# Single-engine steps for attention pieces, row and weight preparation, and PSUM read-outs

## The chip, the core and the metric

The kernel runs on one core of a Trainium2 chip. The metric is the device time of one execution in microseconds (us). A core has TensorE (PE in the profile, its weight loads PEld), VectorE (DVE), ScalarE (ACT), GpSimd (POOL) and SyncE (SP), which here only issues DMAs.

## The reference

2048 tokens of width 1024 go through one layer:

```python
h = rmsnorm(x, attn_norm_w)
q_a, k_a, v_a, q_b, k_b, v_b, g_b, g_c, x_c = split(h @ w_in)   # 1024 -> 3072
y_sb = stick_breaking_attention(q_a, k_a, v_a)                  # 4 heads of 64
y_ch = chunked_relpos_attention(rmsnorm(q_b), rmsnorm(k_b), v_b, rel_bias)   # 8 heads, band of 576 keys
y_cv = g_b * causal_conv3(g_c * x_c)                            # 256 channels
x = x + group_rmsnorm([y_sb, y_ch, y_cv], out_norm_w) @ w_out
x = x + (silu(h2 @ w_gate) * (h2 @ w_up)) @ w_down              # h2 = rmsnorm(x, ffn_norm_w), 2816 wide
```

Stick-breaking attention weights key s by `sigmoid(z_ts)` times the product of `1 - sigmoid(z_tj)` over the keys between s and t; with the sequence stored in reverse order that product is one running product along the keys.

## The kernel before

**Products.** Every projection is made of three half-precision products per 128 rows of the contraction (`mm3`, L320 to L322: high x high, high x low, low x high), in units of 8 x 3 matmuls into an `acc` bank of PSUM (two banks). A weight is two tiles `wr` of 128x1024. `Weights.load` issues their DMAs on SP's queue and, right behind each in ScalarE's program, a Square with a sum (L183) that bounds the tile's size. `Weights.split` adds the sums up on PE (L206 or L208, two small matmuls `ones`), makes a power-of-two scale on VectorE (L212 to L220), and then, for both tiles, scales on ScalarE (L225), casts to the high half (L226), subtracts on GpSimd for the low half (L227), and stores both halves to DRAM (L231). `get` is called when a weight is wanted: it calls `split` of the next weight and `load` of the one after it, in one go.

**Rows.** `Rows.ahead` makes two row blocks of 128 tokens after each other: load, Square (L310), a chain of 11 small VectorE operations (L312 and `rsqrt`, L103 to L116), a multiplication by scale and gain (L314), eight transposes on PE into two `sc` banks (L275, three banks), each read by ScalarE (`hh`, L277) and VectorE (`hl`, L278).

**Attention.** Each of 12 heads is cut into pieces. A piece of stick-breaking attention has three stages: `front` makes scores on PE (L608 to L611), two sigmoids on ScalarE (`be` L634, `re` L635), the running product on VectorE (L636) and a multiplication (L638); `mid` (`transposed`) transposes the result on PE into a `tp` bank (L574, two banks) and reads it by ScalarE (`wth`, L576) and VectorE (`wtl`, L577); `back` multiplies by V into the one `av` bank (L587, L592), which `put_y` reads by ScalarE (L599) and GpSimd adds up (L600). A piece of chunked attention has a maximum (L636's place is taken by L670, L674), an exponential (L676) and a reciprocal (L679, L680). `finish` in `chunk_qk` and `conv_block` transposes into `tp` too (L517, L554).

**Order.** The sequence is cut into two halves. `weave` writes the first 1210 us by hand: `run` takes projection steps from `fill` and counts their cost on a clock; `stage` calls, for one piece after another, `mid` of the piece 3 before, `back` of the piece 5 before and `front` of the piece itself, with a third of a gap of projection steps behind each. `later(t, f)` calls f once the clock has moved by t. In this part PE's order is the written order (`manual_schedule`). The order on VectorE, ScalarE, GpSimd and SP is made by the framework's scheduler from the program as it was written. `y_norm` (L739 to L745) normalizes the first half's attention output between 600 and 760 us. Behind `weave` come the FFN of the first half, the second half's output projection and the second half's FFN; they are not interleaved with attention.

Of the kernel before, what the change touches and what calls it, by code (L numbers as in the profile page):

```python
# [18 lines left out]
D = 1024  # L19
# [21 lines left out]
def trunk(ctx: ExitStack, tc: tile.TileContext, x, anw, w_in, qnw, knw, biasx, conv_w, onw, w_out,  # L41
# [44 lines left out]

    def acc():
        return ps.tile([128, 512], F32, name="acc", tag="acc", bufs=2)

    def sc1():  # L90
        return ps.tile([128, 512], F32, name="sc", tag="sc", bufs=3)

    def tpb():
        return ps.tile([128, 512], F32, name="tp", tag="tp", bufs=2)
# [66 lines left out]
    class Weights:  # L161
# [3 lines left out]
        def __init__(self, plan):  # L165
            self.plan = plan
            self.raw, self.ready = {}, {}
            self.at = 0

        def load(self, n):  # L170
            if n >= len(self.plan) or n in self.raw or self.plan[n] in wd:
                return
            key = self.plan[n]
            shape, one, gain, srcs = block(key)
            ss = small(2, "ws", BF16)
            tiles = []
            for i, unit in enumerate(srcs):
# [7 lines left out]
            self.raw[n] = ss, tiles  # L185

        def split(self, n):
            if n >= len(self.plan) or n in self.ready:
                return
            key = self.plan[n]  # L190
            shape, one, gain, srcs = block(key)
# [9 lines left out]
            ss, tiles = self.raw.pop(n)  # L201
            m = len(tiles)
            o = tpb()
# [5 lines left out]
            c = 1 if one else m  # L209
# [10 lines left out]
            nc.vector.tensor_scalar(ds[:, :c], ds[:, :c], INV[gain], None, op0=ALU.mult)  # L220
            DS[key] = ds, one
            made = []
# [6 lines left out]
            wd[key] = [dp.tile([128, 2, D], F16, name=f"wd{len(wd)}_{i}") for i in range(m)]  # L229
            for w, t in zip(made, wd[key]):  # L230
                nc.sync.dma_start(t, w)  # L231
            self.ready[n] = made

        def ahead(self):
            self.split(self.at)
            self.load(self.at + 1)

        def get(self, key):
# [4 lines left out]
            self.split(n)  # L243
# [23 lines left out]
    def to_T(xn, hh, hl, t):  # L267

        cs = slice(t * 128, (t + 1) * 128)
        for i in range(2):  # L270
            p = sc1()
# [4 lines left out]
            pk = p.rearrange("p (k c) -> p k c", k=4)  # L276
            nc.scalar.copy(hh[:, ks, cs], pk)  # L277
            nc.vector.tensor_tensor(hl[:, ks, cs], pk, hh[:, ks, cs], ALU.subtract)  # L278
            yield 0.45

# [25 lines left out]
    def rms_rows(xt, gain, xo=None):  # L306

        xo = xt if xo is None else xo
        ss = small(1, "ss")
        nc.scalar.activation(junk(), xt, AF.Square, accum_out=ss)  # L310
        a = small(1, "sa")
        nc.vector.tensor_scalar(a, ss, -0.5 / D, -0.5 * EPS, op0=ALU.mult, op1=ALU.add)  # L312
        r = rsqrt(a, 1, "rr")
        nc.vector.scalar_tensor_tensor(xo, xt, r, gain, op0=ALU.mult, op1=ALU.mult)  # L314
        return xo
# [45 lines left out]
    class Rows:  # L361


        def __init__(self, H, groups, make):
            self.H, self.make = H, make
            self.todo = [(g, t) for g in groups for t in (0, 2)]
            self.made = set()
            self.patient = False

        def ahead(self):  # L370
            if self.todo:
# [3 lines left out]
                for b in (t, t + 1):  # L375
                    yield from to_T(self.make(g, b), *self.H[g], b)
# [16 lines left out]
    def x_rows(H, groups):  # L393
        gain = []

        def make(g, b):
# [3 lines left out]
            if not gain:  # L400
                gain.append(gain_row("a"))
            return rms_rows(xt, gain[0])

        return Rows(H, groups, make)

    def y_rows(H, groups):
        def make(g, b):
# [4 lines left out]
        return Rows(H, groups, make)  # L412

    def proj_T(H, groups, u, use, between=None):

        wh, wl = u
        for g in groups:
# [3 lines left out]
            o = acc()  # L421
            yield from mm3(o, lambda k: wh[:, k, :], lambda k: wl[:, k, :], lambda k: hh[:, k, :],
                           lambda k: hl[:, k, :], KT)
            use(g, o)

    def proj_N(H, groups, units, use, prep=None):

        for g in groups:
            hh, hl = H.get(g, (None, None))
            for t in range(0, 4, 2):  # L430
# [3 lines left out]
                o = acc()  # L434
# [6 lines left out]
                use(g, t, o)  # L441
# [45 lines left out]
    def chunk_qk(H, groups, W, pair):  # L487
# [25 lines left out]
        def finish(g, w, both):  # L513
            tp = tpb()
# [3 lines left out]
            put_parts(tp, 2 + pair, g, (qd, kd)[w], nw[:, w:w + 1])  # L518

        yield from proj_N(H, groups, units, use)  # L520

    def conv_block(H, groups, W, b, between=None):
# [28 lines left out]
        def finish(g, t1):  # L551
            tp = tpb()
# [3 lines left out]
            nc.scalar.copy(yc[:, :512], tp)  # L556
            for i in range(4):
# [7 lines left out]
    def transposed(src, n):  # L565
# [3 lines left out]
        for b0, b1 in ([(0, 3), (3, 5)] if n == 5 else [(0, n)]):  # L569
            tp = tpb()  # L570
            s = slice(b0 * 128, b1 * 128)
            c = slice(0, (b1 - b0) * 128)
            for b in range(b0, b1):
                nc.tensor.transpose(tp[:, (b - b0) * 128:(b - b0 + 1) * 128],  # L574
                                    src[:, b * 128:(b + 1) * 128], ident)
            nc.scalar.activation(wh[:, s], tp[:, c], AF.Copy, scale=WSC)  # L576
            nc.vector.scalar_tensor_tensor(wl[:, s], tp[:, c], WSC, wh[:, s], op0=ALU.mult,  # L577
# [19 lines left out]
    def put_y(T, head, av, f):  # L597
        u = ap.tile([128, 2 * HD], F32, name="yu", tag="yu")
        nc.scalar.activation(u, av, AF.Copy, scale=f)  # L599
        nc.gpsimd.tensor_tensor(u[:, :HD], u[:, :HD], u[:, HD:], ALU.add)  # L600
        nc.sync.dma_start(ydr[T][:, head * HD:(head + 1) * HD], u[:, :HD])

    def scores(Q, cols, K, k0, n, diagonal=False):

        q1, q2 = Q
        z = sc1()
# [5 lines left out]
        return z[:, :n]  # L612

    def open_av():
        return ps.tile([128, 2 * HD], F32, name="av", tag="av", bufs=1)

    def stick_tile(T, head, K, k0, Q, V, cols):
# [3 lines left out]
        def piece(b, n):  # L621
            N = n * 128
            r = {}

            def front():
                z = scores(Q, cols, K, (b - k0) * 128, N, b == T)
# [6 lines left out]
                r["w"] = be  # L633
                nc.scalar.activation(be[:, :N], z, AF.Sigmoid, scale=ZS[head // 2][:, 0:1])  # L634
                nc.scalar.activation(re, z, AF.Sigmoid, scale=ZS[head // 2][:, 1:2])  # L635
# [3 lines left out]

            def mid():  # L640
                r["T"] = transposed(r["w"], n)

            def back():
# [3 lines left out]
                weighted(av, *r["T"], [V[:, b + i - k0] for i in range(n)], b == T, b + n == NB)  # L647
                if b + n == NB:
                    put_y(T, head, av, VS[head])

            return front, mid, back, n
# [7 lines left out]
    def chunk_tile(T, head, K, k0, Q, V, cols, bias):  # L659
        n = min(5, NB - T)  # L660
        c0 = (T - k0) * 128
        r = {}

        def front():
# [3 lines left out]
            for i, (a, w) in enumerate(parts):  # L668
                z = scores(Q, cols, K, c0 + a, w)
# [4 lines left out]
            nc.vector.tensor_scalar(nm, m[:, 0:1], other, qks[:, 2:3], op0=ALU.max, op1=ALU.mult)  # L674
            tot = small(1, "tot")
            nc.scalar.activation(s[:, :n * 128], s[:, :n * 128], AF.Exp, bias=nm, scale=qks[:, 1:2],  # L676
                                 accum_out=tot)
            f = small(1, "f")
            nc.vector.reciprocal(f, tot)  # L679
            nc.vector.tensor_tensor(f, f, VS[head], ALU.mult)  # L680
            r["s"], r["f"] = s, f
# [364 lines left out]
```

## Time and profile before

| | before |
|---|---|
| median of 3 executions | 2725.04 us (2721.22 to 2729.78) |
| the profiled execution | 2726.58 us |
| span of its trace | 2724.7 us |
| mean granted clock of PE | 0.98 |
| PE busy | 2539.0 us (93%) |
| DVE, ACT, POOL busy | 1467.3, 1079.9, 401.3 us |

The profiled execution's time is 1.9 us above its span. PE's busy time includes matmuls at the lower of its two clocks, which take twice as long. A row of a timeline gives the start in us from the span's start, the duration, the engine, the line and the operation, its output and inputs, and in brackets how long the engine had been idle and what ended that. Tiles are named by the program; a DMA is named by the tiles at its two ends.

### The profile page before, as it was taken

The numbers are of one execution on the slowest core, as the hardware profiler recorded it, in microseconds if no ns is written. First come the engines' busy times: TensorE is split into PE (matmuls) and PEld (weight loads), VectorE is DVE, ScalarE is ACT, GpSimd is POOL, SyncE is SP. The second block draws the span as 40 slices with busy tenths as digits, with TensorE's granted clock in tenths as the row PEclk, the third lists the DMA queues.
The fourth block names the chain that finished last, engine by engine and source line by source line (L and its number), as shares of the span: only waits on it lengthen the run. The fifth ranks groups of instructions, "written<-read, shape, count | busy, mean of one in ns | idle before, by whom it ended". The sixth has DMA issues, their size and how long they took to land.

```text
span 2724.7 us, 41834 instructions
## 1 busy us (share of the span) xinstructions
PE 2539.0 (93%) x16258; PEld 1690.5 (62%) x16258; DVE 1467.3 (54%) x3455; ACT 1079.9 (40%) x1994; POOL 401.3 (15%) x469
## 2 busy tenths in 40 slices
PE   5988888998799888979999999999999999999999
PEld 4567766766687577845555555556865555555556
DVE  6467877789989877844443334334342333223233
ACT  5566756666466777762333333320121111111110
POOL 2124331112313121121111121110000000000000
PEclk8999999999899999989999999999999999999999
DMA  7443435434221256372222223222651111111101
GB/s 246 142 128 97 124 112 159 129 123 146 92 81 47 97 167 194 94 271 102 93 93 93 93 99 110 93 101 98 226 194 39 47 47 49 68 47 47 47 24 62
DMA packets 245352, 294.34 MB, mean 108 GB/s; under 512 B 77472, under 2 KB 194208, under 8 KB 245152
## 3 DMA queue, kind: packets, MB, share of 16 engines
q1 hardware_dynamic: 245152, 291.65, 33.2%
q8 instruction: 128, 2.10, 0.3%
q14 instruction: 72, 0.59, 0.1%
HBM read 199.30 MB, written 92.27 MB: 107 GB/s over the span
## 4 chain that ended last, share of the span: by engine, by line
PE 37%; DMA 5%; issue 4%; DVE 2%; POOL 1%; ACT 1%; SPq 1%; POOLq 0%; DVEq 0%; ACTq 0%
PE acc L321 7%; PE acc L322 7%; PE acc L320 7%; PE sc L963 5%; PE sc L965 5%; PE sc L964 5%; DMA x1d<-xs 2%; DMA wr<-in_w_down 1%; POOL w L227 1%; DMA wr<-in_w_up 1%; PE sc L275 0%; DVE gl L949 0%; DVE wl L260 0%; DVE x L967 0%; ACT wh L258 0%
## 5 line engine op out<-in xcount | busy, mean ns | idle before, releaser
L321 PE MATMUL acc<-hl,w 128*128 128x512 f16 x1728 | 656.1, 380 | 0.2 <-DVE hl L278 0.2
L320 PE MATMUL acc<-hh,w 128*128 128x512 f16 x1728 | 656.2, 380 | 0.0
L322 PE MATMUL acc<-hh,w 128*128 128x512 f16 x1728 | 655.9, 380 | 0.0
L945 DVE SCALAR_TENSOR_TENSOR sg<-acc,ds,sg 128x512 f32<-128x512 f32 x88 | 66.0, 750 | 614.8 <-PE acc L322 539.5
L320 PE MATMUL acc<-w,hh 128*128 128x256 f16 x1408 | 391.6, 278 | 4.0 <-ACT w L226 4.0
L321 PE MATMUL acc<-w,hh 128*128 128x256 f16 x1408 | 391.6, 278 | 1.8 <-POOL w L227 1.8
L322 PE MATMUL acc<-w,hl 128*128 128x256 f16 x1408 | 391.3, 278 | 0.0
L967 DVE TENSOR_TENSOR x<-sc,x 128x512 f32<-128x512 f32 x352 | 241.4, 691 | 211.0 <-PE sc L965 203.6
L322 PEld LDWEIGHTS <-w 128*128 128x128 f16 x1728 | 169.3, 98 | 205.3 <-issue 2.2
L963 PE MATMUL sc<-wh,gh 128*128 128x512 f32 x704 | 282.3, 401 | 4.6 <-DVE x L967 4.5
L320 PEld LDWEIGHTS <-w 128*128 128x128 f16 x1728 | 169.4, 98 | 183.9 <-issue 5.6
L321 PEld LDWEIGHTS <-w 128*128 128x128 f16 x1728 | 169.3, 98 | 180.1 <-issue 0.6
L965 PE MATMUL sc<-wh,gl 128*128 128x512 f32 x704 | 278.0, 395 | 0.0
L964 PE MATMUL sc<-wl,gh 128*128 128x512 f32 x704 | 277.9, 395 | 0.0
L227 POOL TENSOR_TENSOR w<-wr,w 128x1024 f16<-128x1024 f32 x76 | 162.4, 2157 | 547.1 <-ACT w L226 463.9
L577 DVE SCALAR_TENSOR_TENSOR wtl<-tp,wth 128x512 f16<-128x512 f32 (+3 forms) x384 | 200.2, 530 | 46.9 <-ACT wth L576 45.9
L636 DVE TENSOR_TENSOR_SCAN re<-re,zero 128x512 f32<-128x512 f32 (+3 forms) x160 | 187.7, 1173 | 63.2 <-ACT re L635 63.0
L576 ACT ACTIVATE wth<-tp 128x512 f16<-128x512 f32 (+3 forms) x384 | 176.1, 475 | 81.2 <-PE tp L574 80.2
L948 ACT CAST gh<-sg 128x512 fp32r<-128x512 f32 x88 | 54.3, 617 | 384.4 <-DVE sg L945 384.4
L225 ACT ACTIVATE wr<-wr,wsc 128x1024 f32<-128x1024 f32 x76 | 83.4, 1142 | 194.5 <-DVE wsc L216 194.2
L321 PEld LDWEIGHTS <-hh 128*128 128x128 f16 x1408 | 140.5, 100 | 31.5 <-issue 5.7
L963 PEld LDWEIGHTS sc<-wh,gh 128*128 128x128 f32 x704 | 132.5, 188 | 41.3 <-DVE x L967 8.9
(167 smaller groups left out, 3776.2 us busy)
## 6 DMA issues: line engine op xcount, KB each, us to landing
w<-wd SPq DMA_DIRECT2D x92, 512.0 KB, 4.1
wd<-w SPq DMA_DIRECT2D x76, 512.0 KB, 2.7
wr<-in_w_down SPq DMA_DIRECT2D x44, 512.0 KB, 4.4
q<-qd SPq DMA_DIRECT2D x192, 64.0 KB, 2.3
wr<-in_w_gate SPq DMA_DIRECT2D x22, 512.0 KB, 4.4
wr<-in_w_up SPq DMA_DIRECT2D x22, 512.0 KB, 5.4
xt<-in_x SPq DMA_DIRECT2D x16, 512.0 KB, 4.7
wr<-in_w_in SPq DMA_DIRECT2D x16, 512.0 KB, 5.3
```

What stands on the lines that cost most here:

```text
L225: nc.scalar.activation(raw, raw, AF.Copy, scale=sc[:, 0:1] if one else sc[:, i:i + 1])
L227: nc.gpsimd.tensor_tensor(w[:, 1, :], raw, w[:, 0, :], ALU.subtract)
L320: nc.tensor.matmul(o, sh(k), mh(k), start=(k == 0), stop=False)
L321: nc.tensor.matmul(o, sh(k), ml(k), start=False, stop=False)
L322: nc.tensor.matmul(o, sl(k), mh(k), start=False, stop=(k == n - 1))
L576: nc.scalar.activation(wh[:, s], tp[:, c], AF.Copy, scale=WSC)
L577: nc.vector.scalar_tensor_tensor(wl[:, s], tp[:, c], WSC, wh[:, s], op0=ALU.mult, op1=ALU.subtract)
L636: nc.vector.tensor_tensor_scan(re, re, zero.to_broadcast([128, N]), 1.0 if b == T else e[:, 0:1], ALU.mult, ALU.add)
L963: nc.tensor.matmul(o, gh[:, cs], wh[:, cc], start=st, stop=False)
L964: nc.tensor.matmul(o, gh[:, cs], wl[:, cc], start=False, stop=False)
L965: nc.tensor.matmul(o, gl[:, cs], wh[:, cc], start=False, stop=en)
L967: nc.vector.tensor_tensor(x1, o, x1, ALU.add)
```

## The change

Work that `before` wrote in one go is cut into steps, and what is written between two steps comes between them in the program. A piece is one generator, advanced by `beat`; there are three beats for each new piece. A step holds work of one engine at a time: scores, then both sigmoids (now `re` ahead of `be`), then the running product and the multiplication, and so on. A weight's Squares move from `load` to `split`, which has four steps on the clock (`start`, `more`): Squares; 3.0 later the sum, the scale and, 1.5 after that, the first tile; 1.5 later the second tile. The store of a tile follows its low half at once. Rows are loaded a pair ahead (`fetch`), the two blocks of a pair share one chain of scale operations (`rms_rows`, 15 of them for two rows, where there were 2 x 11), and `to_T` reads a bank one step after its transposes. A projection's `acc` bank is read 0.8 later on the clock (`behind`). `y_norm`'s load is issued 5.0 ahead of its work. `bank` hands out PSUM banks and, where the bank it takes has a reader that is not yet written, writes that reader first. The FFN's functions get the same helpers with nothing deferred.

```diff
+    def bank(name, bufs, cols=512):
+        ring = Bank.rings.setdefault(name, [])
+        if len(ring) == bufs:
+            old = ring.pop(0)
+            while not old.done:
+                old.force() if old.force is not None else advance(old.piece)
+        ring.append(Bank())
+        return ps.tile([128, cols], F32, name=name, tag=name, bufs=bufs), ring[-1]
...
         def load(self, n):
...
                 for put, src in unit:
                     nc.sync.dma_start(put(rv), src)
-                with nc.allow_low_precision(reason="a bound, to a factor of two"):
-                    nc.scalar.activation(junk(), raw, AF.Square, accum_out=ss[:, i:i + 1])
...
         def split(self, n):
...
+            for i, raw in enumerate(tiles):
+                with nc.allow_low_precision(reason="a bound, to a factor of two"):
+                    nc.scalar.activation(junk(), raw, AF.Square, accum_out=ss[:, i:i + 1])
+            yield 3.0
+            o, bk = tpb()
...
             for i, raw in enumerate(tiles):
+                yield 1.5
                 w = wp.tile([128, 2, D], F16, name="w16", tag="w16")
                 nc.scalar.activation(raw, raw, AF.Copy, scale=sc[:, 0:1] if one else sc[:, i:i + 1])
                 nc.scalar.copy(w[:, 0, :], raw)
                 nc.gpsimd.tensor_tensor(w[:, 1, :], raw, w[:, 0, :], ALU.subtract)
+                nc.sync.dma_start(wd[key][i], w)
...
+            run_all(self.steps[n])
             self.load(n + 1)
-            if n:
-                self.ahead()
-            else:
-                later(6.0, self.ahead)
+            self.start(n + 1, 2.0)
+            self.load(n + 2)
...
+    def rms_rows(tiles, gain):
+        a = small(2, "sa")
+        for i, xt in enumerate(tiles):
+            nc.scalar.activation(junk(), xt, AF.Square, accum_out=a[:, i:i + 1])
+        yield 0.0
+        nc.vector.tensor_scalar(a, a, -0.5 / D, -0.5 * EPS, op0=ALU.mult, op1=ALU.add)
+        r = rsqrt(a, 2, "rr")
+        for i, xt in enumerate(tiles):
+            nc.vector.scalar_tensor_tensor(xt, xt, r[:, i:i + 1], gain, op0=ALU.mult, op1=ALU.mult)
+        yield 0.0
...
+    def behind(what):
+        if stream.paced:
+            later(0.8, what)
+        else:
+            what()
...
-            use(g, o)
+            behind(bk.read(lambda g=g, o=o: use(g, o)))
...
-    def transposed(src, n):
+    def turned(src, n):
...
+            for b in range(b0, b1):
+                nc.tensor.transpose(tps[-1][0][:, (b - b0) * 128:(b - b0 + 1) * 128],
+                                    src[:, b * 128:(b + 1) * 128], ident)
+        yield
+        for (tp, bk), (b0, b1) in zip(tps, parts):
+            nc.scalar.activation(wh[:, b0 * 128:b1 * 128], tp[:, :(b1 - b0) * 128], AF.Copy, scale=WSC)
+        yield
...
-                nc.scalar.activation(be[:, :N], z, AF.Sigmoid, scale=ZS[head // 2][:, 0:1])
-                nc.scalar.activation(re, z, AF.Sigmoid, scale=ZS[head // 2][:, 1:2])
+                nc.scalar.activation(re, z, AF.Sigmoid, scale=ZS[head // 2][:, 1:2])
+                nc.scalar.activation(be[:, :N], z, AF.Sigmoid, scale=ZS[head // 2][:, 0:1])
+                yield
...
+        def beat(gap):
+            for p in list(line):
+                p[0] -= 1
+                if p[0] == 0:
+                    advance(p)
+            run(clock[0] + gap / 3)
```

In ScalarE's program at the start, the rows below follow the preparation of the first weight. Rows named `xt` with `junk` are the Squares of token blocks 3 to 8 (L310 before, L368 after), `ws` the Square of a weight (L183, now L249), `hh1` the readers of transposed rows. Before:

```order
L226 CAST w16_305<-wr_286 128x1024
L226 CAST w16_309<-wr_290 128x1024
L310 ACTIVATE junk_384,ss_383<-xt_381 128x1024
L465 ACTIVATE vst_377<-acc_328 128x8x64
L277 CAST hh1_206<-sc_400 128x4x128
L277 CAST hh1_206<-sc_407 128x4x128
L183 ACTIVATE junk_439,ws_436<-wr_437 128x1024
L183 ACTIVATE junk_443,ws_436<-wr_441 128x1024
L225 ACTIVATE wr_318<-wr_318,wsc_417 128x1024
L225 ACTIVATE wr_322<-wr_322,wsc_417 128x1024
```

And after:

```order
L275 CAST w16_299<-wr_277 128x1024
L275 CAST w16_304<-wr_279 128x1024
L368 ACTIVATE junk_374,sa_373<-xt_212 128x1024
L368 ACTIVATE junk_376,sa_373<-xt_214 128x1024
L368 ACTIVATE junk_468,sa_467<-xt_459 128x1024
L368 ACTIVATE junk_470,sa_467<-xt_461 128x1024
L368 ACTIVATE junk_576,sa_575<-xt_463 128x1024
L368 ACTIVATE junk_578,sa_575<-xt_465 128x1024
L249 ACTIVATE junk_761,ws_760<-wr_313 128x1024
L332 CAST hh1_206<-sc_395 128x4x128
```

The Squares of token blocks 4 to 8 moved ahead of everything that the second and third weight need; before, block 4's stood behind two readers, two Squares, two scalings and two casts.

ScalarE's program near 156 us holds attention's rows (`be`, `re`, `wth`, `yu`) mixed with a weight's (`ws`, `wr`, `w16`). Before:

```order
L183 ACTIVATE junk_1784,ws_1780<-wr_1781 128x1024
L634 ACTIVATE be_1718<-sc_1714,zs0_823 128x512
L635 ACTIVATE re_1719<-sc_1714,zs0_823 128x512
L576 ACTIVATE wth_1734<-tp_1736 128x256
L599 ACTIVATE yu_1752<-av_1702,vs0_326 128x128
L183 ACTIVATE junk_1789,ws_1780<-wr_1786 128x1024
L634 ACTIVATE be_1801<-sc_1797,zs0_823 128x512
L635 ACTIVATE re_1802<-sc_1797,zs0_823 128x512
L225 ACTIVATE wr_1563<-wr_1563,wsc_1761 128x1024
L225 ACTIVATE wr_1568<-wr_1568,wsc_1761 128x1024
L226 CAST w16_1768<-wr_1563 128x1024
L226 CAST w16_1772<-wr_1568 128x1024
```

And after, near the same place:

```order
L249 ACTIVATE junk_2249,ws_2246<-wr_1701 128x1024
L694 ACTIVATE yu_1821<-av_1807,vs0_317 128x128
L730 ACTIVATE re_1858<-sc_1824,zs0_739 128x512
L731 ACTIVATE be_1857<-sc_1824,zs0_739 128x512
L548 ACTIVATE vst_1868<-acc_1706 128x8x64
L664 ACTIVATE wth_1850<-tp_1852 128x512
L274 ACTIVATE wr_1474<-wr_1474,wsc_1839 128x1024
L694 ACTIVATE yu_1899<-av_1875,vs0_317 128x128
L275 CAST w16_1891<-wr_1474 128x1024
L730 ACTIVATE re_1858<-sc_1902,zs0_739 128x256
L731 ACTIVATE be_1920<-sc_1902,zs0_739 128x256
L274 ACTIVATE wr_1477<-wr_1477,wsc_1839 128x1024
```

The four long weight operations, which stood in a row, now have attention's operations between them; a weight's Square reads a tile (`wr_1701`) that was loaded long before it in the program, where it stood right behind the load.

## Rows read from the trace of the kernel before

**Rows 1.** The page: busy time of each engine; a costly group (busy, mean ns).

```profile
PE 2539.0 (93%) x16258; PEld 1690.5 (62%) x16258; DVE 1467.3 (54%) x3455; ACT 1079.9 (40%) x1994; POOL 401.3 (15%) x469
...
L320 PE MATMUL acc<-w,hh 128*128 128x256 f16 x1408 | 391.6, 278 | 4.0 <-ACT w L226 4.0
```

**Rows 2.** Windows: length, busy PE, PEld, DVE, ACT, POOL, granted clock, DMA share, GB/s.

```profile
100.00:600.00 500.00, 451.54 (x3779) 331.91 (x3778) 367.99 (x1024) 322.81 (x684) 132.38 (x209) 0.97 0.42 124
600.00:760.00 160.00, 131.47 (x1190) 104.18 (x1187) 156.13 (x319) 90.05 (x167) 47.97 (x44) 0.96 0.35 112
760.00:1210.00 450.00, 393.90 (x3701) 316.36 (x3700) 360.05 (x1023) 312.07 (x638) 102.99 (x147) 0.96 0.42 130
1210.00:2725.00 1515.00, 1495.80 (x7184) 893.80 (x7182) 532.86 (x929) 302.56 (x427) 95.39 (x44) 1.00 0.26 88
```

**Rows 3.** Waits of PE from 0 to 1210: total us, times, longest.

```profile
PE tp L574 <- DVE wtl L577: 41.0, 36, 4.2
PE sc L275 <- DVE xt L314: 27.9, 3, 15.6
...
PE tp L517 <- DVE wtl L577: 10.6, 7, 2.7
...
PE tp L517 <- DVE qrt L111: 6.5, 1, 6.5
```

**Rows 4.** DMA view of the first 16 us.

```profile
DMA packets 3938, 5.06 MB, mean 316 GB/s; under 512 B 144, under 2 KB 3216, under 8 KB 3938
```

**Rows 5.** Timeline of the start.

```profile
20.30 0.37 PE L320 MATMUL acc<-w,hh 128*128 128x256 f16 x1 [4.00 <-ACT w L226]
...
36.81 1.05 ACT L310 ACTIVATE junk<-xt 128x1024 bf16<-128x1024 f32 x1
...
45.55 1.94 PE L275 MATMUL sc<-ident,xt 128*128 128x128 f32 x8 [15.56 <-DVE xt L314]
```

**Rows 6.** Waits of ACT from 100 to 300: total us, times, longest.

```profile
ACT junk L183 <- DMA wr<-in_w_in: 19.1, 9, 3.7
```

**Rows 7.** Timeline, 155 to 295: ACT and PE around weights' Squares.

```profile
155.99 1.06 ACT L183 ACTIVATE junk<-wr 128x1024 bf16<-128x1024 f32 x1 [3.67 <-DMA wr<-in_w_in]
...
160.01 0.87 PE L574 MATMUL tp<-ident,be 128*128 128x128 f32 x3 [3.79 <-DVE wtl L577]
...
294.09 0.55 PE L574 MATMUL tp<-ident,be 128*128 128x128 f32 x3 [0.73 <-DVE wtl L577]
```

**Rows 8.** Timeline, 151 to 980: ACT and PE around weights' scalings and casts.

```profile
151.07 0.63 PE L554 MATMUL tp<-ident,t 128*128 128x128 f32 x4 [1.21 <-DVE wtl L577]
...
228.18 2.19 ACT L225 ACTIVATE wr<-wr,wsc 128x1024 f32<-128x1024 f32 x2
...
230.26 1.99 ACT L226 CAST w<-wr 128x1024 f16<-128x1024 f32 x2
...
235.39 0.47 PE L574 MATMUL tp<-ident,be 128*128 128x128 f32 x1 [4.21 <-DVE wtl L577]
...
979.08 0.80 PE L574 MATMUL tp<-ident,s 128*128 128x128 f32 x5 [1.38 <-DVE f L679]
```

**Rows 9.** Timeline: PE behind a row block's Square.

```profile
1059.04 1.02 PE L574 MATMUL tp<-ident,s 128*128 128x128 f32 x5 [4.65 <-DVE f L679]
```

**Rows 10.** Windows with the lower clock, columns as in Rows 2.

```profile
158.50:165.00 6.50, 4.99 (x26) 3.84 (x27) 4.54 (x10) 6.50 (x11) 1.72 (x3) 0.50 0.28 69
233.50:240.00 6.50, 4.61 (x26) 3.47 (x27) 5.54 (x13) 1.63 (x3) 4.84 (x4) 0.50 0.38 121
...
916.20:922.80 6.60, 5.30 (x25) 3.95 (x26) 5.47 (x8) 2.03 (x4) 0.86 (x3) 0.50 0.78 274
```

**Rows 11.** Timeline: a GpSimd operation and a VectorE operation beside it.

```profile
350.53 2.13 POOL L227 TENSOR_TENSOR w<-wr,w 128x1024 f16<-128x1024 f32 x1 [3.33 <-ACT w L226]
...
350.91 1.77 DVE L111 TENSOR_TENSOR qrt<-qrt,qa 128x16 f32<-128x16 f32 x1
```

**Rows 12.** Waits of PE from 1184 to 1210.

```profile
PE sc L275 <- DVE xf L314: 11.5, 4, 5.3
```

More of the change, by code (lines that the diff above doesn't have):

```diff
@@ L85, in trunk, with __init__, read, once @@
     ynd = [dp.tile([128, D], F32, name=f"ynd{t}") for t in range(NB)]
+    class Bank:
+        rings = {}
+        def __init__(self):
+            self.done = False
+            self.piece = running[0]
+            self.force = None
+        def read(self, what):
+            def once():
+                if not self.done:
+                    self.done = True
+                    what()
+            self.force = once
+            return once
+    running = [None]
+    def bank(name, bufs, cols=512):
[6 more added lines that the diff above has]
+        return ps.tile([128, cols], F32, name=name, tag=name, bufs=bufs), ring[-1]
     def acc():
-        return ps.tile([128, 512], F32, name="acc", tag="acc", bufs=2)
+        return bank("acc", 2)
     def sc1():
-        return ps.tile([128, 512], F32, name="sc", tag="sc", bufs=3)
+        return bank("sc", 3)
     def tpb():
-        return ps.tile([128, 512], F32, name="tp", tag="tp", bufs=2)
+        return bank("tp", 2)
+    def advance(p):
+        before, running[0] = running[0], p
+        wait = next(p[1], "over")
+        running[0] = before
+        if wait == "over":
+            line.remove(p)
+            traced[p[2]] -= 1
+        else:
+            p[0] = wait or 1
+    line = []
+    traced = [None, None]
     def small(n, name, dt=F32):
@@ L200, in split @@
             self.load(n)
-            ss, tiles = self.raw.pop(n)
+            shape, one, gain, srcs = block(key)
+            tiles = self.raw.pop(n)
+            self.ready[n] = made = []
             m = len(tiles)
-            o = tpb()
+            c = 1 if one else m
+            ss = small(2, "ws", BF16)
+            for i, raw in enumerate(tiles):
[3 more added lines that the diff above has]
+            o, bk = tpb()
             if one:
@@ L227, in split, with start, more @@
                 nc.gpsimd.tensor_tensor(w[:, 1, :], raw, w[:, 0, :], ALU.subtract)
+                nc.sync.dma_start(wd[key][i], w)
                 made.append(w)
[L229 to L236, printed above, removed]
+        def start(self, n, after=0.0):
+            self.steps[n] = self.split(n)
+            if self.paced:
+                later(after, lambda: self.more(n))
+            else:
+                run_all(self.steps[n])
+        def more(self, n):
+            after = next(self.steps[n], None)
+            if after is not None:
+                later(after, lambda: self.more(n))
         def get(self, key):
@@ L374, in ahead @@
                     self.H[g] = hcols(g)
-                for b in (t, t + 1):
-                    yield from to_T(self.make(g, b), *self.H[g], b)
+                tiles = self.get(g, t)
+                if t == 0:
+                    self.get(g, 2)
+                if self.norm is not None:
+                    yield from self.norm(tiles)
+                for b, xt in zip((t, t + 1), tiles):
+                    yield from to_T(xt, *self.H[g], b)
+                del self.got[g, t]
                 self.made.add((g, t))
@@ L391, in beside, with normed, norm, fetch @@
             yield from more
+    def normed(key):
+        gain = []
+        def norm(tiles):
+            if not gain:
+                gain.append(gain_row(key))
+            yield from rms_rows(tiles, gain[0])
+        return norm
     def x_rows(H, groups):
-        gain = []
-        def make(g, b):
+        def fetch(g, b):
             xt = xp.tile([128, D], F32, name="xt", tag="xt")
@@ L556, in finish @@
             nc.scalar.copy(yc[:, :512], tp)
+            bk.done = True
             for i in range(4):
@@ L646, in back @@
                 av = state["av"]
-                weighted(av, *r["T"], [V[:, b + i - k0] for i in range(n)], b == T, b + n == NB)
+                weighted(av[0], *w, [V[:, b + i - k0] for i in range(n)], b == T, b + n == NB)
                 if b + n == NB:
-                    put_y(T, head, av, VS[head])
-            return front, mid, back, n
+                    yield from put_y(T, head, av, VS[head])
+            return steps(), n
         b = T
```

200 lines of the change are left out of this document (98 added, 102 removed).

## The prediction

> **What bounds the kernel now.** I read the page first. PE is busy 2539 of 2725 us [rows 1], so at most some 186 us are to be had from waits, and what matters is where they lie. The windows answer that: from 1210 on PE is busy 1495.8 of 1515 us at full clock [rows 2], and the change defers nothing there, so I take no gain and no loss behind 1210. In the interleaved part PE is idle 48.5 us between 100 and 600, 28.5 between 600 and 760, and 56.1 between 760 and 1210 [rows 2]; the start is read by itself below. In none of these windows is the granted clock 1.00 [rows 2]: stretches of 3.4 to 7 us run at 0.50, the lower of the two levels, 1.2 GHz.
>
> The grouped waits then say whom PE waits for. The largest group, 41 us in 36 waits, has a transpose wait for `wtl`, VectorE's reader of a transpose bank [rows 3]. VectorE is not the cause by itself outside 600 to 760 (busy 368 of 500 us between 100 and 600, but 156 of 160 in that window [rows 2]): `wtl` waits for ScalarE's `wth`, and `wth` stands behind something in ScalarE's queue. So I went through the timeline at these waits and looked for what ScalarE did 4 to 9 us earlier. Two things recur. A weight's Square waits for its DMA with attention's operations queued behind it: nine such waits, 19.1 us, between 100 and 300 [rows 6]. And a weight's four long operations run in a row, 2.19 + 1.99 = 4.2 us, while PE runs dry [rows 8].
>
> **The start.** PE waits 15.56 us at 45.55 for the normalized token block 4, whose Square ran only at 36.81 [rows 5]. In the order before, two readers, two Squares, two scalings and two casts of the next weight stand ahead of it; after, it is the second operation behind the first weight's casts. From that Square to the transposes 8.7 us went by (36.81 to 45.55). PE had work from 20.30 to 30.0 (45.55 less 15.56). Against this, four blocks are loaded ahead of the first weight where two were: two more loads of 512 KB, at 316 GB/s [rows 4] 1.66 us each, so the first product comes at 23.6 and PE's 9.7 us of work end at 33.3. Block 4's Square starts one Square (1.05) behind the casts, at about 24.7, and with the same 8.7 us its transposes could begin at 33.4 to 34.4. Left of the 15.6 are 3.3 + 1.1: the term is **-11**. Bounds: -6, if the four Squares behind delay the next weight's casts by their 4.2 us; -14, if the loads overlap what hid them before.
>
> At this place stands something that speaks against the change. A VectorE operation on 16 elements took 1.77 us beside a GpSimd subtraction, and both ended at 352.7 [rows 11]. The chain for a pair of rows now has products of two small tiles (n is 2, so `rsqrt` takes its other branch), like that operation, and it runs while GpSimd makes the first weight's two low parts. The Trainium skill ("SBUF — State Buffer", section "Who interferes with whom") says that a VectorE instruction with two SBUF inputs contends with a GpSimd instruction that reads SBUF, and that the loser is blocked for the whole instruction. The trace agrees, with the 1.77 us. By that rule the chain starts some 2 us later, when the second low part ends (two of 2.13 us, against two Squares of 1.05), and this term would be -9.
>
> **Weights on ScalarE.** The Squares now stand where the data have long landed, so the DMA waits go. Behind five of them PE waited, from 3.79 us at 160.01 to 0.73 at 294.09 [rows 7], 9.2 us together. The four long operations are separated: after, attention's `wth`, `yu`, `re` and `be` stand between them (the order near 156 us). Behind eight of the thirteen such bursts between 100 and 1010, PE waited ten times, from 1.21 us at 151.07 to 1.38 at 979.08, 4.21 at 235.39 among them [rows 8], 23.0 us together. A row block's Square that waited for its own DMA held ScalarE in the same way before the 4.65 us wait at 1059.04 [rows 9]; rows are now loaded a pair ahead. That makes 36.9 us of waits with a cause that is removed. Not all of it comes back: an operation of 1.1 us still stands ahead of `wth`, and PE is up to 4 us early for the next wait. I take 70%: **-26**. Bounds: -12 (a third: the next wait ends as late) and -37.
>
> **The clock.** Three stretches at 0.50 lie at such waits, at 158.5, 233.5 and 916.2, with 4.99, 4.61 and 5.30 us of PE's work each [rows 10]; at full clock half of it, 2.3 to 2.7 us, goes. PE waited 3.79 us up to 160.01 and 4.21 up to 235.39 [rows 7, 8]; where it does not wait, I expect the clock to stay. Three such stretches and a short one make **-8**; bounds 0 (the clock falls elsewhere) and -16 (twice as many).
>
> **600 to 760.** Here VectorE is the bound, 156 of 160 us [rows 2], because `y_norm` comes on top. No VectorE work of size is removed, but in the new order attention's `wtl` and `be` stand ahead of parts of `y_norm`, and its loads are issued early. The work itself has to be done before the output projection, with slack from 760 on (VectorE 360 of 450 us). I take **-4** of the 28.5 idle us; bounds 0 and -15.
>
> **Transposes of q and k.** `finish` moves back by 6 to 9 projection matmuls, some 2 us at 0.278 each [rows 1], against waits of 10.6 and 6.5 us for `wtl` and `qrt` [rows 3]. **-3**; bounds +4 (pieces then get q and k later) and -10.
>
> **Into the FFN.** PE waits 11.5 us for the first rows of the FFN [rows 12]. They are loaded ahead now, but a pair is transposed only after both Squares and a shared chain: **-2**; bounds +5 and -8.
>
> **What is new.** A weight is ready later, since its steps are spread over the clock. From the Square to the low part there are 1.06 (Square), 1.09 and 1.00 (scaling and cast, half of a pair [rows 8]) and 2.13 us [rows 11], 5.3 us, and where the order leaves the least room, 21 matmuls stand between the sum and the first use, 5.9 us at 0.28 with attention's between: at one or two of the 17 weights PE may wait some 3 us. A reader one step later holds its PSUM bank longer, in rings of two and three. Reading `re` ahead of `be` and about 110 fewer small VectorE operations give something back, in places where VectorE mostly has time. I take **+9** for all new waits; bounds +2 and +25.
>
> **The sum.** -11 - 26 - 8 - 4 - 3 - 2 + 9 = **-45** against the profiled execution's 2726.6: 2681.6. That execution stands 1.5 above the median, so 2680 for the median.
>
> **Rivals.**
> 1. *More comes back.* With ScalarE's queue clear, VectorE's backlog in 600 to 760 dissolves too, and the clock stays up in most stretches: the upper bounds of three terms (-37, -16, -15) in place of -26, -8 and -4, with the rest as it is, give -75: 2650, and 2625 at the far end. For it: `wtl` is the releaser in most waits of PE. Against: from 600 to 760 no work goes away. 0.15.
> 2. *A small gain.* The start's term holds, but of the waits only a third comes back and the clock none: -11 - 12 - 2 + 10 = -15, some 2710 (2702 to 2717). For it: a wait for ScalarE may be followed by one as long for VectorE, `yu` or the score banks. 0.10.
> 3. *The change doesn't do what it says.* PE's order is nearly the old one; the scheduler may have filled the engines as well before, and what the steps spread out is released at the same times. Then only the start changes, less what is new: -11 + 9, about 2723 (2717 to 2733). Against it: the order of ScalarE does differ, at the places of the waits. 0.08.
> 4. *Slower.* The spread preparation of a weight becomes the wait: scaling and cast stand singly in ScalarE's queue behind `wth`, `yu` and the sigmoids, which themselves wait for PE, so that each of the 17 weights' chains of 5.3 us is stretched to over 10, and PE waits at its first matmul some 5 us, with a stretch at the lower clock of 2.4: 17 x 7.4 = 126 in full, about 2760 if it strikes at two thirds of them (-45 + 84). It decides from where the mean wait per weight passes 45/17 = 2.6 us. For it: before, a weight was ready one whole weight ahead. Against it: most sums stand 69 matmuls (19 us) ahead of the first use. 0.07.
>
> **How the numbers follow.** The main case, 2660 to 2702, gets 0.60: two of the large terms (-26, +9) at their bounds one at a time move it by no more than 16. With 0.15 for more, 0.10 for small, 0.08 for none and 0.07 for slower the range must leave out no more than 2 in 10: 2645 to 2712 cuts off half of the first rival, a part of the second, and the last two. A measurement of this kernel tells 0.3%, 8 us, from no change: faster takes the main case and rivals 1 and 2, 0.85; same is rival 3, 0.08; slower rival 4, 0.07.
>
> **What would show it.** In the new profile: the wait for `xt` at the start below 5 us and the first product at 22 to 24; no wait of ScalarE's weight Squares for a DMA between 100 and 1210; the group of `tp` waiting for `wtl` below 25 us; the granted clock of 100 to 600 at 0.98 or more; PE idle between 100 and 600 at 25 to 35; the window behind the weave as long as before. I am wrong if PE waits for `w` (scaling, cast or low part) or the `acc` and `sc` banks by more than 15 us in all, or if waits for `wtl` stay at 41 with another operation ahead of `wth`.

## The result and the profile after

The changed kernel ran at 2696.1 us (median of 4; 2693.0 to 2698.6) against 2723.3 for the kernel before on the same chips: a ratio of 0.9896, 95% interval 0.9874 to 0.9917, so 23 to 34 us faster. Forecast were 2680 (2645 to 2712). The profiled execution took 2698.6 us, its span 2696.8.

The page and the windows of the changed kernel, columns as in [rows 1, 2]:

```profile
PE 2526.3 (94%) x16258; PEld 1687.1 (63%) x16258; DVE 1458.7 (54%) x3343; ACT 1074.8 (40%) x1994; POOL 398.8 (15%) x469
...
100.00:600.00 500.00, 459.05 (x3848) 336.73 (x3847) 381.03 (x1012) 327.36 (x695) 133.35 (x209) 0.97 0.42 125
600.00:760.00 160.00, 127.83 (x1146) 103.41 (x1144) 152.94 (x318) 84.93 (x157) 49.18 (x44) 0.93 0.36 116
760.00:1210.00 450.00, 395.00 (x3691) 313.47 (x3690) 352.71 (x979) 310.27 (x638) 97.81 (x146) 0.97 0.44 135
```

PE's busy time fell by 12.7 us although it does the same 16258 matmuls, and the clock is no better than before. Idle time and clock can't account for that alone. Windows at fixed times hold different work in two kernels, so I counted the products of the projections and the FFN (the matmuls of `mm3`, which stand in the same order in all kernels here) and noted when the same one starts. Numbers from 0; the last column is the last less number 4608, which is the second product after the weave's end:

```
kernel            0      288     1152     2304     4608     9407    last part
before         20.3     88.2    279.2    599.1   1237.9   2675.3    1437.4
after          22.7     79.7    265.4    583.6   1224.0   2648.1    1424.1
a_undoW        23.0     86.7    279.5    597.6   1242.4   2668.5    1426.2
a_undoR        20.3     77.3    260.5    580.2   1220.1   2642.8    1422.7
a_onlyA        20.2     89.9    280.6    601.2   1246.8   2671.0    1424.2
a_burst        22.6     79.6    270.9    594.2   1232.6   2655.6    1423.0
a_hold         24.8     88.0    261.7    580.1   1207.4   2642.4    1435.0
b_onlyW        20.4     77.9    264.4    584.5   1211.8   2636.0    1424.1
a_best         20.4     77.7    251.8    565.4   1194.1   2616.6    1422.5
b_best         20.5     79.0    255.1    566.2   1187.9   2609.2    1421.3
b_pad_ffn384   20.4     89.9    280.6    600.3   1233.7   2654.9    1421.2
b_pad_all384   20.4     89.8    281.5    602.2   1239.3   2664.1    1424.7
b_pad_ffn128   20.4     89.9    281.7    603.9   1242.9   2667.0    1424.1
a_pad_ffn128   22.9     79.8    263.1    582.4   1223.3   2654.5    1431.2
```

Before to after: 8.5 us gained by number 288, 13.8 by 1152, 15.5 by 2304, 13.9 by 4608, and another 13.3 behind it, where the change defers nothing. (The kernels whose weave is that of before, the first and the three b_pad, reach 4608 at 1233.7 to 1242.9: one profile tells a stage to some 5 us.)

The last part has a plain trace. The matmuls of the down projection, before and after (count, busy, mean ns, idle before):

```profile
L964 PE MATMUL sc<-wl,gh 128*128 128x512 f32 x704 | 277.9, 395 | 0.0
```

```profile
L1058 PE MATMUL sc<-wl,gh 128*128 128x512 f32 x704 | 274.4, 390 | 0.0
```

All three lines became 5 ns shorter with nothing waited for: 2112 x 5 ns = 10.6 us.

### The profile page after: what moved, and what is told of

Same layout as the page of the kernel before. It is cut to its first block, busy times and chain, and to the rows that moved or that the text cites. A ratio compares the mean times of both kernels' runs of the same rounds, so it can differ in the third digit from the quotient of the medians.

```text
span 2696.8 us, 41816 instructions
## 1 busy us (share of the span) xinstructions
PE 2526.3 (94%) x16258; PEld 1687.1 (63%) x16258; DVE 1458.7 (54%) x3343; ACT 1074.8 (40%) x1994; POOL 398.8 (15%) x469
## 4 chain that ended last, share of the span: by engine, by line
PE 38%; DMA 4%; issue 4%; DVE 2%; POOL 1%; ACT 1%; SPq 1%; POOLq 0%; DVEq 0%; ACTq 0%
PE acc L381 7%; PE acc L380 7%; PE acc L379 7%; PE sc L1057 5%; PE sc L1058 5%; PE sc L1059 5%; DMA x1d<-xs 1%; POOL w L276 1%; DMA wr<-in_w_down 1%; DMA wr<-in_w_up 1%; DMA xf<-x1d 0%; PE sc L329 0%; DVE gl L1042 0%; DVE x L1061 0%; DVE wl L314 0%
## 5 line engine op out<-in xcount | busy, mean ns | idle before, releaser
L679 PE MATMUL av<-v,wth 128*128 128x128 f16 x1104 | 144.0, 224 | 16.3 <-ACT yu L694 16.2
```

Source lines behind the costliest of these rows:

```text
L679: nc.tensor.matmul(av, wh[:, i * 128:(i + 1) * 128], vs[i], start=first and i == 0, stop=last and i == n - 1 > 0)
```

## The experiments

All keep the rest of the kernel that they start from. Names with b_ start from the kernel before, with a_ from the changed one; times are medians beside runs of the kernel before on the same chip (2723.3 to 2723.9).

**The FFN's gain: where its tiles stand.** `rms_rows` lost its tile `ss` of 128 bytes per partition (four buffers), and everything allocated behind it moved down by that much: the FFN's tiles stood 128 bytes past a multiple of 512 and now stand at one. The padding (the comment is added here):

```diff
+    pp = ctx.enter_context(tc.tile_pool(name="pp", bufs=1))
+    pad = pp.tile([128, 96], F32, name="pad")      # 384 bytes; 32 elements for 128
+    nc.vector.memset(pad, 0.0)
     fp = ctx.enter_context(tc.tile_pool(name="fp", bufs=1))
```

> The kernel before, with an unused tile of 384 bytes per partition ahead of the FFN's tiles alone, so that they start at a multiple of 512 bytes as in the changed kernel (before: 128 bytes past one). Nothing is reordered. Theory P (place): the 13 us that the changed kernel gained behind 1217 are mostly its matmuls of the down projection, whose mean time fell from 395 to 390 ns (2112 of them, spaced 232 and 227 ns), because the tile that was dropped (ss) moved the FFN's tiles by 128 bytes. Then this kernel gains 10 to 12 us, all behind 1217, and the weave stays as it was. Rival O (order): the FFN's gain comes from the order of rows, weights or read-outs there. Then this kernel runs as before, within 2 us.

> The changed kernel, with 128 bytes per partition ahead of the FFN's tiles, so that they stand where they stood before. Theory P: it loses 10 to 12 us of its 27, and the down projection's matmuls are back at 395 ns. Rival O: it keeps all 27.

> The kernel before, with the 384 bytes ahead of attention's tiles too, which also stood 128 bytes past a multiple of 512. Theory P: as with the FFN's tiles alone, plus whatever attention's transposes and products gain by their place; with reads of at most 512 bytes and some 3 us of matmul time per 1 percent I expect 0 to 4 us more. Rival O: as before.

 (The tile stands in the pool `sp`, ahead of attention's and the FFN's pools.)

> The kernel before, with 128 bytes ahead of the FFN's tiles, so that they start 256 bytes past a multiple of 512. Theory P does not say whether a multiple of 256 is enough. If it is, this gains the same 10 to 12 us as 384 bytes; if it takes a multiple of 512, the matmuls stay near 395 ns and the time at that of before. Rival O: as before.

Measured: 2714.9, 2705.1, 2714.5 and 2713.5 us, ratios 0.9970 (0.9958 to 0.9982), 0.9933 (0.9920 to 0.9947), 0.9969 (0.9960 to 0.9978) and 0.9962 (0.9950 to 0.9975). The line of the down projection in b_pad_ffn384 and in a_pad_ffn128:

```profile
L967 PE MATMUL sc<-wl,gh 128*128 128x512 f32 x704 | 274.3, 390 | 0.0
```

```profile
L1061 PE MATMUL sc<-wl,gh 128*128 128x512 f32 x704 | 277.9, 395 | 0.0
```

So the kernel before gains 9 us by the padding alone, and the changed kernel loses 9 when its tiles go back to the old place: theory P holds, 1 us short of its 10 to 12, and O falls. Standing 256 bytes past a multiple of 512 does as well as standing at one (b_pad_ffn128), and attention gains nothing from it (b_pad_all384). What is left for the new order is 2714.5 less 2696.1, some 18 us.

**Which steps carry the 18 us.** The edits in short (each line stands for the whole of `Weights` or `Rows` as it was before; in a_undoR the transposes' banks are read at once, too):

```diff
 a_undoW, in Weights:
-    yield 3.0    # and: yield 1.5, start(), more()
+    self.split(n); self.load(n + 1)    # load, split, ahead, get as before
 a_undoR, in Rows.ahead:
-    yield from self.norm(tiles)
+    for b in (t, t + 1):
+        xt = self.fetch(g, b); self.norm(xt); yield from to_T(xt, *self.H[g], b)
```

> The changed kernel with the weights prepared as before: Square written behind each load, sum, scale and both tiles in one go. Tiles stand where they stand in the changed kernel. My prediction's theory W: spreading a weight's steps is the largest term in the weave; then this kernel loses most of what the weave gained from 100 on, 6 to 10 us, and runs at 2702 to 2706. Rival H (hoisting): ScalarE's order is the scheduler's, which puts a Square back to where it takes its load to be there, so that the steps changed little (Squares waited 24.7 us for DMAs between 100 and 1210 in the changed kernel, 19.3 before, and scalings 16.8 for VectorE, 7.5 before). Then it runs within 4 us of 2696.

> The changed kernel with rows as before: each block loaded, squared and scaled by itself, banks read at once; 384 bytes of padding keep attention's and the FFN's tiles at multiples of 512 bytes. Theory R: the start's 8.5 us come from the order of the rows' Squares and loads; then this kernel loses 8 to 11 us, at the start, and the wait for xt there is back at some 15 us behind the first product. Rival: the start moved for another reason (read-outs, weights in steps); then it keeps the 8.5 us.

> Attention's steps alone: the changed kernel with weights, rows, read-outs and the load of y_norm as before, padded so that tiles stand at multiples of 512 bytes. Against the kernel before with the same padding (2714.5): theory A0, the pieces' steps change little, since PE's order is nearly the old one and the other engines' is the scheduler's in both: within 4 us of 2714.5. Rival A1: they carry the weave's gain from 100 on: 2706 to 2710.

Measured: a_undoW 2714.6 (0.9964, 0.9951 to 0.9977), a_undoR 2693.3 (0.9885, 0.9864 to 0.9906), a_onlyA 2718.4 (0.9974, 0.9962 to 0.9985). Without the weights' steps nothing is left of the 18 us: rival H falls as to the time (what it says of the Squares comes back below), and theory W had the loss at about half its size. With rows as before the kernel is no slower, and the start keeps its gain (number 288 at 77.3), so my theory R falls too. Attention's steps alone bring nothing.

Where the start's gain comes from, PE's longest waits for a row block (`xt`) behind the first product help to show. In a_undoR and a_undoW they are:

```profile
44.25 0.63 PE L331 MATMUL sc<-ident,xt 128*128 128x128 f32 x4 [1.21 <-DVE xt L374]
```

```profile
47.94 1.09 PE L320 MATMUL sc<-ident,xt 128*128 128x128 f32 x4 [4.74 <-DVE xt L364]
```

With the weights' steps, rows as before wait 1.2 us (and 2.3 at another block, for `rry` of the rows' chain); with weights as before, rows in pairs still wait 4.7 (it was 15.6 [rows 5]). With either of the two the long wait for block 4 is gone, but only the weights' steps bring the time: number 288 starts at 77.3 in a_undoR and at 86.7 in a_undoW, where other waits stand in its place (3.2 us for `hh` at 39.9) and the first product comes later. Rows in pairs have a price, the first product at 22.69 instead of 20.30:

```profile
22.69 0.37 PE L379 MATMUL acc<-w,hh 128*128 128x256 f16 x1 [4.15 <-ACT w L275]
```

The reverse experiment, the weights' steps alone on the kernel before (with 384 bytes of padding for the FFN):

> The kernel before with the weights' steps alone (rows, attention and read-outs as before), and 384 bytes ahead of the FFN's tiles. Theory W1: the weights' steps carry the whole gain of the new order, since taking them out of the changed kernel cost 18.5 us. Then it runs at 2694 to 2700, with the start's 15.6 us wait for xt gone although the rows are as before. Rival X: the steps only pay together with attention's; then it runs at 2706 to 2714, as the padded kernel before did (2714.9).

Measured: 2684.9 (0.9863, 0.9849 to 0.9876). It is better than the whole change: 30 us less than the same padding without it (2714.9), and 11 less than the changed kernel. Rival X falls; theory W1 had the steps carry the whole gain, and they carry more than that. With these steps in place the other parts cost 11 us; without them they cost nothing (a_undoW 2714.6 against 2714.5 for the padded kernel before). So the parts don't simply add up: the weights' steps are worth 30 us alone and 18.5 in the changed kernel.

**What of the weights' steps: bursts or waits for loads.** Between 100 and 1010 us scaling, scaling, cast, cast stand in a row 11 times in the trace of before, once in that of the changed kernel, and 7 times with this edit:

```diff
 a_burst
+            yield 1.5
             for i, raw in enumerate(tiles):
-                yield 1.5
                 w = wp.tile([128, 2, D], F16, name="w16", tag="w16")
```

> The changed kernel with both tiles of a weight scaled and cast in one step, 1.5 behind the sum, where it has 1.5 between the tiles; Squares stay in steps. Scaling, scaling, cast, cast then stand in a row on ScalarE again for most weights. Theory B: the bursts of 4.2 us are what the steps removed; then it loses 6 to 10 us (2702 to 2706). Rival S: what pays is that a weight's operations come later than in the kernel before, single or not; then it stays within 4 us of 2696.

Measured: 2707.9 (0.9947, 0.9935 to 0.9960), 11.8 us lost, a little more than theory B asked; up to number 288 nothing is lost, and 8.6 us by 4608. PE's largest groups of waits from 0 to 1210 in a_burst, and in the changed kernel:

```profile
PE tp L660 <- DVE wtl L669: 59.2, 34, 6.3
...
PE tp L600 <- DVE wtl L669: 16.8, 8, 5.7
```

```profile
PE tp L660 <- DVE wtl L669: 54.4, 37, 4.6
...
PE sc L329 <- DVE xf L373: 13.2, 2, 9.5
PE tp L600 <- DVE wtl L669: 11.9, 7, 2.9
```

The waits for loads, which I had expected to go, are there still. ScalarE's waits from 100 to 1210 in the kernel before, and in the changed kernel:

```profile
ACT junk L183 <- DMA wr<-in_w_in: 19.3, 10, 3.7
...
ACT wr L225 <- DVE wsc L216: 7.5, 9, 1.8
```

```profile
ACT junk L249 <- DMA wr<-in_w_in: 24.7, 10, 6.3
...
ACT wr L274 <- DVE wsc L263: 16.8, 10, 4.2
```

And one of them in its timeline, SP, ScalarE and PE:

```profile
204.26 0.32 SPq L277 DMA_DIRECT2D wd<-w  x1
204.99 0.32 SPq L697 DMA_DIRECT2D ydr<-yu  x1
205.36 1.62 SPq L223 DMA_DIRECT2D wr<-in_w_in  x3
...
210.98 1.06 ACT L249 ACTIVATE junk<-wr 128x1024 bf16<-128x1024 f32 x1 [5.83 <-DMA wr<-in_w_in]
...
212.04 0.58 ACT L664 ACTIVATE wth<-tp 128x512 f16<-128x512 f32 x1
212.51 0.36 ACT L694 ACTIVATE yu<-av,vs 128x128 f32<-128x128 f32 x1
...
212.92 0.27 PE L679 MATMUL av<-v,wth 128*128 128x128 f16 x1 [2.78 <-ACT yu L694]
```

ScalarE sits 5.83 us at a Square whose load was issued only at 205.4, `wth` and `yu` behind it, and PE waits. The Square is written a weight's time behind its load, but its place on ScalarE is the scheduler's, and the load is issued late. In SP's queue it stands behind two stores, which GpSimd released at 204.2 (`wd`, the halves of a weight's tile) and at 205.0 (`ydr`). Whether a store further back in that queue would spare the wait was not tried. This edit keeps the written order on ScalarE (the comments are added here):

```diff
+    def behind(self, n):
+        if n < 3 or not self.paced:        # a_hold: for all weights
+            return contextlib.nullcontext()
+        return tc.issue_after(next(i for i in reversed(nc.cur_bb.bb.instructions)
+                                   if i.engine == mybir.EngineType.Activation))
...
+        with self.behind(n):               # around the Squares, and around scaling and cast
```

> The changed kernel with each weight's Squares, and each tile's scaling and cast, queued on ScalarE behind the operation of ScalarE that was written last ahead of them (an order without a wait), so that the scheduler can't move them up. Theory H: ScalarE's waits for weight loads and scales, 24.7 and 16.8 us between 100 and 1210, fall below 10 together, and of the waits of PE behind them some go: 4 to 10 us faster than the changed kernel. Rival: these waits are not what PE waits for; then the waits fall, and the time stays within 4 us of 2696. A third: held back, weights come late; then PE waits for w, and it is slower.

> The changed kernel with rows as before, and the Squares, scalings and casts of weights from the fourth on kept in written order on ScalarE, in the interleaved part only; padded so that tiles stand at multiples of 512 bytes. With rows as before the changed kernel ran at 2693.3; the order kept on all weights ran at 2691.8, with 16.7 us gained up to the FFN in its profile and 11 lost behind. Theory H: the two add up, some 2676 to 2684. Rival: what was gained up to the FFN is scatter of one profile; then 2690 to 2694.

> The kernel before with the weights' steps, and from the fourth weight on their Squares, scalings and casts kept in written order on ScalarE in the interleaved part; 384 bytes ahead of the FFN's tiles. Attention, rows and read-outs are as before. The weights' steps alone ran at 2684.9, and the written order gave 21.5 us where attention was in steps too (2671.8 against 2693.3). Theory: the two add up without attention's steps, 2660 to 2668. Rival: with attention's stages in one go the written order finds less to stand between; then 2670 to 2685, no better than 2671.8, and attention's steps are worth something once weights keep their place.

Measured: a_hold 2691.8 (0.9873, 0.9853 to 0.9894): 16.6 us ahead of the changed kernel at number 4608, but its start lost 8.3 us and its last part takes 10.9 longer. ScalarE's waits for weight loads are gone there; those for the scale fell only to 12.2, so that theory H's "below 10 together" was missed, and 4.3 us is the low end of its range. Held only where attention is interleaved, and not for the first weights, with rows as before, a_best runs at 2671.8 (0.9813, 0.9796 to 0.9830), and with attention as before too, b_best at 2662.8 (0.9781, 0.9763 to 0.9800): 4 us below the range that was expected for a_best, and inside that for b_best. Windows of a_best and b_best:

```profile
100.00:600.00 500.00, 466.84 (x4017) 347.00 (x4014) 397.18 (x1067) 338.52 (x717) 132.40 (x210) 0.99 0.42 125
```

```profile
100.00:600.00 500.00, 464.08 (x4001) 345.52 (x3999) 387.12 (x1074) 340.23 (x717) 134.97 (x212) 0.99 0.42 127
```

In a_best no Square of these weights waits for `in_w_in` between 100 and 1210. Of ScalarE's waits at weights these are left:

```profile
ACT wr L284 <- DVE wsc L272: 12.1, 9, 3.2
...
ACT junk L258 <- DMA wr<-in_w_gate: 1.7, 1, 1.7
```

Here 466.8 of 500 us are busy at clock 0.99, and 4017 matmuls were done where it was 3848 in the changed kernel. The written order is worth 21.5 us (2693.3 to 2671.8) with attention in steps and 22.1 (2684.9 to 2662.8) without: theory H holds as to a cause. PE's waits for `wtl` at the pieces' transposes fell along with it, from 52.3 us (a_undoR) to 40.2 and from 36.7 (b_onlyW) to 23.2. As Squares, scalings and casts are all held, it isn't shown which of them carries how much. And attention's steps, with the deferred read-outs and the earlier load of `y_norm`, cost 8.4 (2693.3 against 2684.9) and 9.0 us (2671.8 against 2662.8), alike in both pairs. What PE waits for more with them are the transposes' banks, here in a_best and in b_best:

```profile
PE tp L666 <- DVE wtl L675: 40.2, 39, 4.9
...
PE tp L666 <- DVE be L741: 5.0, 2, 3.1
```

```profile
PE tp L592 <- DVE wtl L595: 23.2, 24, 3.2
...
PE tp L592 <- DVE be L656: 11.0, 7, 3.4
```

For `wtl`, the reader of such a bank, it is 17.0 us more, for `be`, what is transposed, 6.0 less. A bank's reading one step later than its filling would do that; it was not tried by itself, nor were the read-outs apart from attention's steps.

## Why the prediction was right, and where not

Direction and range held; of the -45 us, 27 came, and 9 of these from something that I had not seen. That the number lies in the range is in part luck. With the FFN's tiles where they stood before, the changed kernel runs at 2705.1 (a_pad_ffn128): outside the main case (2660 to 2702), and inside the 2702 to 2717 of rival 2, in which the start's term holds, few of the waits come back and the clock gives nothing. That is also what the profile shows. Of the signs that were named, only those of the start came (first product at 22.69, longest wait for `xt` behind it 2.19). The Squares' waits stayed, the clock from 100 to 600 is 0.97, PE is idle there for 41 us and not for 25 to 35, and the waits for `wtl` at the pieces' transposes rose from 41.0 [rows 3] to 54.4 us, which had been named as a sign of being wrong.

- **Behind 1210**, "no gain and no loss", was wrong: -13.3 in the two profiles, some -9 of it by the place of the FFN's tiles. The trace of before can't show this; only the program's addresses could have.
- **The start**, -11: measured -8.5 by number 288. The wait for block 4 went, as I said (2.19 us at 41.43, for a later block, is the longest left behind the first product). But the time came with the weights' operations leaving ScalarE, not with the rows in pairs; these cost 2.4, where I had put 3.3 for the loads. The prediction took the rule on the shared port from the Trainium skill ("SBUF — State Buffer", section "Who interferes with whom"). The new chain does not test it: the products of two small tiles ran once GpSimd was done, and took 0.16 us each. The operation that was stretched was the first one, with a single tile input, which ended with GpSimd's at 26.9:

```profile
22.72 4.21 POOL L276 TENSOR_TENSOR w<-wr,w 128x1024 f16<-128x1024 f32 x2 [20.75 <-DMA nw<-in_q_norm_w]
...
25.84 1.12 DVE L370 TENSOR_SCALAR sa<-sa 128x2 f32<-128x2 f32 x1 [2.52 <-ACT junk L368]
```

  That is some 1 us (1.12 against 0.17 for the operation behind it) where I had put 2, and at another operation.
- **Weights on ScalarE**, -26, is the term that failed, by half or more. The weights' steps are worth 18.5 us in the changed kernel (a_undoW), and 7.0 of these had come by number 288; that leaves 11.5. From 288 to 4608 the whole weave gained 5.4 us net. The bursts were a cause, and not far from their price: 23.0 of the 36.9 us were theirs, 16 at 70%, and a_burst, which brings most of them back, loses 11.8. The Squares had 9.2 of the 36.9, some 6 at 70%, and of these "the Squares now stand where the data have long landed, so the DMA waits go" did not happen: ScalarE waited 24.7 us for `in_w_in` from 100 to 1210 and 16.8 for the scale, where it had been 19.3 and 7.5. I read the place of a Square in the new order as time, and did not look at when its load is issued. Once the written order is held, the load waits go (in a_best most of those for the scale stay), and 22 us come, over three times that price. So I had undervalued the order on ScalarE, and the change did not bring it about.
- **The clock**, -8: 0.97 from 100 to 600 in both, 0.96 to 0.93 from 600 to 760. It rose to 0.99 from 100 to 600 in a_best and b_best, where PE waits less.
- **600 to 760**, -4: PE's idle time there is 32.2 us (160 less 127.8), not less than 28.5; VectorE still is the bound (152.9 of 160).
- **q and k**, -3: the wait for `wtl` at L600 is 11.9 us (10.6 before); the 6.5 us for `qrt` is gone, and one of 4.1 for `qry` at L660 is new. The "2 us at 0.278 each" took the duration of a product for the distance to the next. They overlap, and start 0.11 us apart in the trace of before:

```profile
25.35 0.27 PE L320 MATMUL acc<-w,hh 128*128 128x256 f16 x1
25.46 0.27 PE L321 MATMUL acc<-w,hh 128*128 128x256 f16 x1
```

  So 6 to 9 of them are under 1 us, and the 21 and 69 matmuls under "What is new" and rival 4 are 2.3 and 7.5 us, not 5.9 and 19, as far as they are such products.
- **Into the FFN**, -2: 13.2 us in 2 waits, the longest 9.5, against 11.5 in 4 [rows 12]: a loss of some 2, within the bound.
- **What is new**, +9: about right in size (11 us, by b_onlyW), but not where I looked for it: PE hardly waits for weights, and the cost lies in attention's steps and read-outs (8 to 9 us) and the pairs of rows (2.4 at the start).

From run to run, the way from the kernel before to the changed one is -9 for the place, -30 for the weights' steps (b_onlyW) and +11 for the rest. The last is what is left over, so that this sum closes by itself and is no proof of its parts.

## What to carry to other kernels

Where a scheduler orders an engine, writing a step later does not by itself place it later on the chip: look at when the data's load is issued and what stands ahead of it in its queue, and pin the order where an engine queues other work behind a wait. Measure the parts of a mixed change apart; here one part was worth more than the whole. And before a gain is put down to an order, see whether an unrelated stage changed its speed: a tile dropped from a pool moves all that is allocated behind it.

## What the hardware showed unexpectedly

Matmuls of 128x512 in f32 type took 395 ns and stood 232 ns apart where the FFN's tiles began 128 bytes past a multiple of 256 bytes in their partition, as in the kernel before and a_pad_ffn128, and 390 and 227 ns where they began at such a multiple, in the changed kernel and b_pad_ffn384 (a multiple of 512) and in b_pad_ffn128 (256 past one). Of these matmuls' operands only `gh` and `gl`, which are loaded as weights, stand in the FFN's pool; `wh` and `wl` stand in `wp`, ahead of all that moved. So the place of `gh` and `gl` is the likely cause; they were not moved by themselves.
